# Two transformer blocks under a list scheduler: a longer assumed load time, finer priority offsets, and a last output in two pieces

## The chip, the cores and the metric

The kernel runs on one core of one Trainium2 chip. A core has TensorE (PE) for matmuls and transposes, VectorE (DVE), ScalarE (ACT), GpSimd (POOL), and SyncE (SP), which here issues nearly all DMA transfers. Every engine takes its instructions in a fixed order and waits on semaphores. The metric is the device time of one execution in microseconds.

## The reference, cut to what matters

The input is 256 tokens of 1024 columns, batch 1, float32. It goes through two layers of a first block and then two layers of a second one.

```python
# first block, per layer
mod = silu(c) @ w_ada[l] + b_ada[l]                  # 6 x 1024
hdn = modulate(rmsnorm(x, norm1_g[l]), shift1, scale1)
proj = hdn @ w_in[l]     # q_lat 768, c_kv 256, k_pe 32, sb_qkv 1536, mb_qkv 1536, gates 3072
q  = rmsnorm(q_lat) @ w_uq[l];  kv = rmsnorm(c_kv) @ w_ukv[l]
o_mla = softmax attention with rope;  o_sb = stick-breaking attention;  o_mb = block attention
merged = g_a * (o_mla @ w_o_mla) + g_b * (o_sb @ w_o_sb) + g_c * (o_mb @ w_o_moba)
x = x + gate1 * (merged @ w_out[l])
x = x + gate2 * (relu(modulate(rmsnorm(x, norm2_g[l])) @ w_ff1[l])**2 @ w_ff2[l])   # d_ff 4096
# then a final rmsnorm. Second block, per layer: modulation of x and of a context (256 tokens),
# one input projection, then branches for attention, Fourier, convolution and pooling over the
# tokens, concatenated to `cat`, and x = x + gate * (cat @ w_out_2[l]); the last layer ends with x.
```

## The kernel before, in words

Every float32 matmul is done as three matmuls of split operands: `mm3` multiplies high by high, high by low and low by high parts. A weight tile goes through three steps in `wload` (L600): a DMA into `raw`, a cast on ACT into `whi`, and a subtraction on DVE into `wlo`. PE then reads `whi` and `wlo`. Modulation vectors are made by "fillers" (`filler_step`, L752): loads `araw` and accumulations `acc` on DVE, let in between the weight loads at the rate `RATE`.

The Python code doesn't issue instructions. It records operations (`Recorder.add`, L228), and a list scheduler (`class Scheduler`, L320) gives each a start time and each tile a slot in SBUF (40 large, 11 half, 40 small) or PSUM (4 and 4 banks). `emit` (L444) then writes them out by start time, and so the order of each engine's instructions is set. All instructions carry its line: L464 before, L454 after. The scheduler's `forward` takes the ready operation with the smallest priority number. An operation's priority is its latest start in the last `backward` pass less its `lead`, an offset from the table `LEAD` (L1785) by `part` and `stage` of the code that recorded it (the stages are named `lat`, `up`, `att sb`, `gates`, `ff` and so on, with the layer's number). `LAG` (L329) is what the scheduler adds between an operation on an engine and one that needs its result. Its times are its own; the chip keeps only the orders.

Names used below: `sq_lat` and `lat` are the square sums and copies of the latent projections `g`; `ssv_ql` and `xn_ql` are the norm's small steps on DVE, and `nT_ql`, `nT_kvl` the transposes of the normed latents on PE. `s_sb`, `p_sb`, `pT_sb`, `pTs_sb` are scores, weights, transposed weights and their copies in stick-breaking attention. `gc` is a gate projection. `f`, `fr`, `f1T` are feed-forward products, the relu on ACT and their transposes. `tl_zc`, `cy` and `ct` are the convolution branch on DVE, and `cat0h`, `cat0l` its split result. `yt` and `gh` belong to the Fourier branch. The last product is `ev` in the second layer (L1700 to L1719): each 512 output columns of a token tile are multiplied by the gate, added to `x` and sent out by one DMA.

Of the kernel before, what the change touches and what calls it, by code (L numbers as in the profile page):

```python
# [18 lines left out]
ALU = mybir.AluOpType  # L19
# [148 lines left out]
class Recorder:  # L168
# [61 lines left out]
    def add(self, eng, fn, args, kw):  # L230
        if self.group:
            op = self.group[0]
        else:
            op = Op(len(self.ops), eng, fn, args, kw)
            op.lead = 0.0 if eng == "sync" else LEAD.get(self.part, 0.0) + LEAD.get(self.stage, 0.0)
            self.ops.append(op)
            if self.group is not None:
                self.group.append(op)
# [81 lines left out]
class Scheduler:  # L320
# [7 lines left out]
    LAG = {"tensor": 200.0, "vector": 150.0, "scalar": 150.0, "gpsimd": 100.0, "sync": 1000.0}  # L328
# [95 lines left out]
    def run(self, passes):  # L424

        best = None
        prio = list(range(len(self.ops)))
        for _ in range(passes):
            t = self.forward(prio)
            if best is None or t < best[0]:  # L430
                best = (t, [(op.start, op.end) for op in self.ops], [b.slot for b in self.bufs], self.edges)
            prio = [t - op.lead for t, op in zip(self.backward(), self.ops)]
        self.restore(best)
        return best[0]

    def restore(self, state):
        for op, (s, e) in zip(self.ops, state[1]):
            op.start, op.end = s, e
        for b, s in zip(self.bufs, state[2]):
            b.slot = s  # L440
        self.edges = state[3]
# [61 lines left out]
def record(nc, a, out):  # L503
# [102 lines left out]
    def wload(w2d, r0, nk, c0, n, eng=None, sort=0):  # L606


        uid[0] += 1
        parts = []  # L610
# [19 lines left out]
        filler_tick(nk * n / 2048.0)  # L630
        return parts
# [120 lines left out]
    def filler_step():  # L752
        nc.stage, stage = "ada", nc.stage
        try:
# [3 lines left out]
        nc.stage = stage  # L758
# [677 lines left out]
    def second_layer(l, late, hT):  # L1436
# [281 lines left out]
        gemm_tok(cat, 8, a["w_out_2"][l], [(512, 512)], lambda t, _, p: ev(t, 1, p), toks=toks, stag=True)  # L1718
        return h_next  # L1719
# [57 lines left out]
    for l in range(L):  # L1777
# [7 lines left out]
PASSES = 3  # L1785
RATE = 0.4354
LEAD = {"norm": 2550.0, "lead": 2700.0, "lead weights": 2950.0, "residual": -1660.0, "sb": -8810.0, "ml": -16600.0,
# [48 lines left out]
```

## Time and profile before

| | us |
|---|---|
| three runs | 1307.62, 1313.01, 1315.68 (median 1313.01) |
| the profiled execution | 1312.1 |
| its span, first to last instruction | 1310.1 |
| PE busy | 1270.7 (97%) |
| DVE busy | 1044.5 (80%) |
| ACT busy | 727.0 (55%) |
| POOL busy | 85.0 (6%) |

The span is about 2 us shorter than the execution it belongs to. PE is busy nearly all the time, so what matters is where PE stood idle or ran at a lower clock, and what ended each such stretch. In the profile's windows PEclk is the granted clock of TensorE: 1.00 is its 2.4 GHz level and 0.50 its 1.2 GHz level.

### The profile page before, as it was taken

To read this page: it belongs to the slowest core of one execution; us is meant where nothing else is said; L and a number is where in the kernel's file an instruction comes from. 1 tells how busy PE (TensorE), PEld (TensorE's weight loads), DVE (VectorE), ACT (ScalarE), POOL (GpSimd) and SP (SyncE) were. 2 spreads that over 40 slices of the span, in tenths; PEclk is the share of its full clock that TensorE was granted. 3 is DMA by queue.
4 is the path that set the end of the run, shared out by engine and by line. 5 is a ranking of instruction groups with operands and counts; after the bars stand their busy time and mean duration, and the time that the engine had idled before them with its cause. 6 is when DMAs were issued, how large, how long until landed. Compare 5 with 4: busy or idle time off the path is not lost. (4 is left out here: it accounts for less than half of the span.)

```text
span 1310.1 us, 21962 instructions
## 1 busy us (share of the span) xinstructions
PE 1270.7 (97%) x8258; PEld 1116.8 (85%) x8258; DVE 1044.5 (80%) x1705; ACT 727.0 (55%) x1246; POOL 85.0 (6%) x112
## 2 busy tenths in 40 slices
PE   6899999999999999999999999999999999999998
PEld 4898888997889888999889988889888777788997
DVE  4878988977966676888788978988878769967875
ACT  6576756645654554677566556545645453335661
POOL 1000000110000000100001200000001014100120
PEclk9898999999999999999999999999999999999999
DMA  8966565676688856775666766887744314824631
GB/s 293 354 231 206 173 215 193 224 241 227 212 319 271 282 186 203 251 235 180 205 219 194 250 226 228 284 294 238 250 140 150 105 35 163 276 79 134 218 105 38
DMA packets 164192, 272.68 MB, mean 208 GB/s; under 512 B 26395, under 2 KB 57071, under 8 KB 164086
## 3 DMA queue, kind: packets, MB, share of 16 engines
q1 hardware_dynamic: 164086, 271.28, 61.8%
q8 instruction: 65, 1.06, 0.3%
q14 instruction: 41, 0.34, 0.1%
HBM read 270.11 MB, written 1.13 MB: 207 GB/s over the span
## 5 line engine op out<-in xcount | busy, mean ns | idle before, releaser
L464 ACT CAST whi<-raw 128x1024 fp32r<-128x1024 f32 (+3 forms) x354 | 351.8, 1014 | 247.3 <-DMA raw<-w_ff 44.0
L464 DVE TENSOR_TENSOR wlo<-raw,whi 128x1024 fp32r<-128x1024 f32 (+3 forms) x354 | 412.5, 1195 | 38.3 <-ACT whi L464 33.1
L464 DVE SCALAR_TENSOR_TENSOR acc<-araw,cT,acc 128x1024 f32<-128x1024 f32 x147 | 190.2, 1313 | 37.8 <-DMA araw<-w_ada 26.5
L464 PE MATMUL gc<-hT1h,whi 128*128 128x256 f32 x256 | 74.0, 289 | 0.0
L464 PE MATMUL gc<-hT1h,wlo 128*128 128x256 f32 x256 | 71.9, 281 | 0.0
L464 PE MATMUL gc<-hT1l,whi 128*128 128x256 f32 x256 | 71.9, 281 | 0.0
L464 PE MATMUL f<-fT0h,whi 128*128 128x256 f32 x192 | 54.2, 282 | 0.0
L464 PE MATMUL f<-fT1l,whi 128*128 128x256 f32 x192 | 54.1, 282 | 0.0
L464 PE MATMUL f<-fT1h,whi 128*128 128x256 f32 x192 | 54.0, 281 | 0.0
L464 PE MATMUL f<-fT1h,wlo 128*128 128x256 f32 x192 | 54.0, 281 | 0.0
L464 PE MATMUL f<-fT0l,whi 128*128 128x256 f32 x192 | 53.9, 281 | 0.0
L464 PE MATMUL f<-fT0h,wlo 128*128 128x256 f32 x192 | 53.8, 280 | 0.0
L464 PE MATMUL cb<-h20h,whi 128*128 128x512 f32 x128 | 53.6, 419 | 0.0
L464 PE MATMUL gc<-hT0h,whi 128*128 128x256 f32 x176 | 51.7, 294 | 0.0
L464 PE MATMUL cb<-h20h,wlo 128*128 128x512 f32 x128 | 50.5, 394 | 0.0
L464 PE MATMUL cb<-h20l,whi 128*128 128x512 f32 x128 | 50.4, 394 | 0.0
L464 PEld LDWEIGHTS gc<-hT1h,whi 128*128 128x128 f32 x256 | 48.4, 189 | 2.1 <-issue 1.9
L464 PE MATMUL gc<-hT0l,whi 128*128 128x256 f32 x176 | 49.4, 281 | 0.0
L464 PE MATMUL gc<-hT0h,wlo 128*128 128x256 f32 x176 | 49.3, 280 | 0.0
L464 PEld LDWEIGHTS gc<-hT1l,whi 128*128 128x128 f32 x256 | 48.4, 189 | 0.0
L464 PEld LDWEIGHTS gc<-hT1h,wlo 128*128 128x128 f32 x256 | 48.3, 189 | 0.0
L464 PE MATMUL g<-whi,hT1h 128*128 128x512 f32 (+1 forms) x112 | 43.4, 388 | 0.0
(643 smaller groups left out, 3834.9 us busy)
## 6 DMA issues: line engine op xcount, KB each, us to landing
raw<-w_ff SPq DMA_DIRECT2D x128, 512.0 KB
raw<-w_in SPq DMA_DIRECT2D x126, 512.0 KB
araw<-w_ada SPq DMA_DIRECT2D x96, 256.0 KB
araw<-w_ada SPq DMA_DIRECT2D x32, 512.0 KB
raw<-w_out SPq DMA_DIRECT2D x32, 512.0 KB
araw<-w_mod SPq DMA_DIRECT2D x64, 256.0 KB
raw<-w_in SPq DMA_DIRECT2D x24, 352.0 KB
araw_l<-lead_ada SPq DMA_DIRECT2D x32, 256.0 KB
```

The lines of the kernel that those rows point to most:

```text
L464: op.inst.append(getattr(getattr(nc, op.eng), fn)(*[val(x) for x in args], **{k: val(x) for k, x in kw.items()}))
```

## The change

The scheduler assumes 3932 ns between a load and its first reader where it assumed 1000. Loads get offsets too, an operation's offset is now the sum of those of its part, its stage and its stage on its engine, and the three steps of `wload` form a part "weights" of their own; fillers belong to no part. All offsets have new values. `run` makes five passes and keeps the last instead of the best of three, and `RATE` is a little higher. In the last layer the last 512 columns of the second token tile are computed, gated, added and sent out as two pieces of 256 columns (24 matmuls of 512 columns become 48 of 256; DVE gets two instructions more, SP one DMA more).

```diff
--- before.py
+++ after.py
@@ -232,7 +232,8 @@
             op = self.group[0]
         else:
             op = Op(len(self.ops), eng, fn, args, kw)
-            op.lead = 0.0 if eng == "sync" else LEAD.get(self.part, 0.0) + LEAD.get(self.stage, 0.0)
+            op.lead = 0.0 if eng == "sync" else sum(
+                LEAD.get(q, 0.0) for q in (self.part, self.stage, f"{self.stage}/{eng}"))
             self.ops.append(op)
             if self.group is not None:
                 self.group.append(op)
@@ -325,7 +326,7 @@
                 self.ops[p].succs.append(op.idx)
         self.bufs = rec.bufs
 
-    LAG = {"tensor": 200.0, "vector": 150.0, "scalar": 150.0, "gpsimd": 100.0, "sync": 1000.0}
+    LAG = {"tensor": 200.0, "vector": 150.0, "scalar": 150.0, "gpsimd": 100.0, "sync": 3932.0}
 
     def lag(self, a, b, raw=True):
 
@@ -423,22 +424,11 @@
 
     def run(self, passes):
 
-        best = None
         prio = list(range(len(self.ops)))
-        for _ in range(passes):
-            t = self.forward(prio)
-            if best is None or t < best[0]:
-                best = (t, [(op.start, op.end) for op in self.ops], [b.slot for b in self.bufs], self.edges)
-            prio = [t - op.lead for t, op in zip(self.backward(), self.ops)]
-        self.restore(best)
-        return best[0]
-
-    def restore(self, state):
-        for op, (s, e) in zip(self.ops, state[1]):
-            op.start, op.end = s, e
-        for b, s in zip(self.bufs, state[2]):
-            b.slot = s
-        self.edges = state[3]
+        for i in range(passes):
+            if i > 0:
+                prio = [t - op.lead for t, op in zip(self.backward(), self.ops)]
+            self.forward(prio)
 
 
 def emit(tc, ctx, rec):
@@ -607,6 +597,7 @@
 
 
         uid[0] += 1
+        nc.part, part = "weights", nc.part
         parts = []
         step = max(1, 1024 // n)
         for j in range(0, nk, step):
@@ -628,6 +619,7 @@
                 (eng or nc.vector).tensor_tensor(l_, r_, h_.bitcast(F32), op=ALU.subtract)
             parts.extend((hv[:, i], lv[:, i]) for i in range(m))
         filler_tick(nk * n / 2048.0)
+        nc.part = part
         return parts
 
 
@@ -751,11 +743,12 @@
 
     def filler_step():
         nc.stage, stage = "ada", nc.stage
+        nc.part, part = None, nc.part
         try:
             next(filler[0][1])
         except StopIteration:
             filler.pop(0)
-        nc.stage = stage
+        nc.stage, nc.part = stage, part
 
     def filler_tick(n):
         rate[1] += n * rate[0]
@@ -1715,8 +1708,20 @@
                     second_norm(l + 1, "c", xc[t - 2], ss[t], t, h_next)
 
         gemm_tok(cat, 8, a["w_out_2"][l], [(0, 512)], ev, toks=toks)
-        gemm_tok(cat, 8, a["w_out_2"][l], [(512, 512)], lambda t, _, p: ev(t, 1, p), toks=toks, stag=True)
-        return h_next
+        if full:
+            gemm_tok(cat, 8, a["w_out_2"][l], [(512, 512)], lambda t, _, p: ev(t, 1, p), toks=toks, stag=True)
+            return h_next
+
+        ws = wload(a["w_out_2"][l], 0, 4, 512, 512) + wload(a["w_out_2"][l], 512, 4, 512, 512)
+        for t, c0, n in ((0, 512, 512), (1, 512, 256), (1, 768, 256)):
+            p = MM(f"end{t}{c0}")[:, 0:n]
+            for k, (wh, wl) in enumerate(ws):
+                c = slice(c0 - 512, c0 - 512 + n)
+                mm3(p, cat.h(k)[:, tok(t)], cat.l(k)[:, tok(t)], wh[:, c], wl[:, c], k == 0, k == 7)
+            tmp, sl = S2(f"rt_end{t}{c0}", n), slice(c0, c0 + n)
+            nc.vector.tensor_tensor(tmp, p, gate_bc[("x", l)][:, sl], op=ALU.mult)
+            nc.vector.tensor_tensor(x[:, t, sl], x[:, t, sl], tmp, op=ALU.add)
+            nc.sync.dma_start(out=out[0, t * 128:(t + 1) * 128, sl], in_=x[:, t, sl])
 
 
     for l in range(L):
@@ -1782,16 +1787,48 @@
 
 SLOTS = {"s4": 40, "s2": 11, "sm": 40, "mm": 4, "tr": 4}
 CAPS = {"w": 24, "r": 8}
-PASSES = 3
-RATE = 0.4354
-LEAD = {"norm": 2550.0, "lead": 2700.0, "lead weights": 2950.0, "residual": -1660.0, "sb": -8810.0, "ml": -16600.0,
-        "mb": -6240.0, "attention2": -17800.0, "ada": 3060.0, "att mb0": -190.0, "att mb1": -1340.0,
...
-        "up1": 770.0, "z att0": 5800.0, "z att1": 620.0}
+PASSES = 5
+RATE = 0.4386
+LEAD = {"None/sync": -6220.0, "None/tensor": -670.0, "None/vector": -290.0, "ada/sync": 8040.0, "att mb0": -60.0,
+        "att mb0/scalar": 290.0, "att mb0/tensor": 2280.0, "att mb0/vector": 110.0, "att mb1": -690.0,
+        "att mb1/scalar": 660.0, "att mb1/tensor": -90.0, "att mb1/vector": -10.0, "att ml0/scalar": -2180.0,
...
+        "up1/vector": -2950.0, "z att0": -318.0, "z att0/scalar": 260.0, "z att0/sync": -3760.0,
+        "z att0/vector": 1350.0, "z att1": 40.0, "z att1/tensor": -500.0, "z att1/vector": -200.0}
```

Three places show how the orders move.

**Place 1: up0, the latent norm of the first layer.** PE, from the end of the latent projection `g` to the transposes `nT_ql` and `nT_kvl`. Before (the left-out rows repeat the pair of `s_sb`):

```order
L464 MATMUL g_10_1031<-whi_2_924,hT0l_513 128x352
L464 MATMUL s_sb_1133<-kssb_811,qssb_780 128x128
L464 MATMUL s_sb_1133<-k_low_73,qssb_780 128x128
...
L464 MATMUL nT_ql_1163<-ct,xn_ql_1151 128x128 x4
L464 MATMUL nT_ql_1172<-ct,xn_ql_1151 128x128 x2
L464 MATMUL nT_kvl_1188<-ct,xn_kvl_1161 128x128 x2
L464 MATMUL nT_kvl_1198<-ct,xn_kvl_1192 128x128 x2
L464 MATMUL g_00_1207<-whi_0_955,laT0h_1186 128x384
```

And now:

```order
L454 MATMUL g_10_1027<-whi_2_973,hT0l_514 128x352
L454 MATMUL s_sb_1120<-kssb_799,qssb_773 128x128 x3
L454 MATMUL gc_0_1124<-hT0h_198,whi_0_1078 128x256
L454 MATMUL gc_0_1124<-hT0l_205,whi_0_1078 128x256
L454 MATMUL gc_0_1124<-hT0h_198,wlo_0_1094 128x256
L454 MATMUL s_sb_1120<-kssb_799,qssb_773 128x128
L454 MATMUL gc_0_1124<-hT0h_198,whi_0_1078 128x256
L454 MATMUL gc_0_1124<-hT0l_205,whi_0_1078 128x256
L454 MATMUL gc_0_1124<-hT0h_198,wlo_0_1094 128x256
L454 MATMUL s_sb_1120<-k_low_75,qssb_773 128x128 x4
L454 MATMUL nT_ql_1157<-ct,xn_ql_1137 128x128 x4
L454 MATMUL nT_ql_1164<-ct,xn_ql_1137 128x128 x2
```

Two groups of three `gc` stand among the eight `s_sb` ahead of `nT_ql`. ACT at the same place, up to the square sums and copies of that projection. Before (`whi_0_1029` is a cast for the product behind the norm, `gt` a gate activation):

```order
L464 CAST whi_0_1029<-raw_0_1003 128x768
L464 ACTIVATE sq_lat_1040,sl_13_1041<-g_11_978 128x352
L464 ACT_TABLE_LOAD
...
L464 COPY lat_1055<-g_11_978 128x352
L464 CAST whi_0_1079<-raw_0_1043 128x2x256 x2
L464 CAST whi_0_1097<-raw_0_1064 128x2x256 x2
L464 ACTIVATE sq_lat_1115,sl_14_1116<-g_00_1025 128x64
```

And now:

```order
L454 CAST whi_0_1060<-raw_0_986 128x2x256 x2
L454 CAST whi_0_1078<-raw_0_1007 128x1024
L454 ACT_TABLE_LOAD
L454 ACTIVATE rope_c<-rope_c 128x48
L454 CAST whi_2_1096<-raw_2_1025 128x768
L454 ACTIVATE sq_lat_1106,sl_14_1107<-g_00_1018 128x64
...
L454 COPY lat_1016<-g_10_1027 128x320
L454 CAST whi_0_1153<-raw_0_1044 128x768
```

The cast `whi_0_1029` of before is `whi_0_1153` now, and stands behind the last copy `lat` instead of ahead of the square sums. Ahead of the first of these square sums are now a cast in two pieces, one of 1024 columns, a table load with the `rope_c` activation, and one of 768 columns. The order of ACT has 9 table loads where it had 8.

**Place 2: the convolution branch of the second block's first layer.** DVE, up to the first `tl_zc`. Before:

```order
L464 SCALAR_TENSOR_TENSOR cy_12472<-tl_cc_12343,vt,cy_12472 128x2x255 x2
L464 TENSOR_TENSOR wlo_2_12495<-raw_2_12410,whi_2_12443 128x1024
L464 TENSOR_TENSOR wlo_0_12505<-raw_0_12420,whi_0_12470 128x1024
L464 TENSOR_TENSOR wlo_2_12517<-raw_2_12436,whi_2_12497 128x1024
L464 TENSOR_TENSOR wlo_0_12529<-raw_0_12457,whi_0_12510 128x1024
L464 SCALAR_TENSOR_TENSOR acc_0_12382<-araw_2_12512,cT,acc_0_12382 128x1024
L464 SCALAR_TENSOR_TENSOR tl_zc_12556<-th_zc_12548,cb_2048_0_12438 128x512
L464 SCALAR_TENSOR_TENSOR tl_zc_12556<-th_zc_12558,cb_2048_1_12445 128x512
```

And now:

```order
L454 SCALAR_TENSOR_TENSOR cy_12468<-tl_cc_12337,vt,cy_12468 128x2x255 x2
L454 TENSOR_TENSOR wlo_0_12482<-raw_0_12363,whi_0_12431 128x1024
L454 TENSOR_TENSOR wlo_2_12495<-raw_2_12380,whi_2_12466 128x1024
L454 TENSOR_TENSOR wlo_0_12507<-raw_0_12390,whi_0_12490 128x1024
L454 TENSOR_SCALAR acc_0_12514<-araw_0_12426,cT 128x1024
L454 TENSOR_TENSOR wlo_2_12519<-raw_2_12403,whi_2_12500 128x1024
L454 SCALAR_TENSOR_TENSOR tl_zc_12540<-th_zc_12529,cb_2048_0_12442 128x512
L454 SCALAR_TENSOR_TENSOR tl_zc_12540<-th_zc_12542,cb_2048_1_12447 128x512
```

The order at the place is almost the same; an accumulation with a multiply and add has become one with a multiply alone. By the operations counted from the start, tl_zc is row 1281 of DVE's order and was row 1289.

**Place 3: stick-breaking attention in the second layer.** ACT, from the copy of one transposed weight tile to that of the next. Before:

```order
L464 COPY pTs_sb_7005<-pT_sb_6988 128x512
L464 ACTIVATE gt_6986<-gc_1_6721 128x512
L464 COPY rr_7017<-rs_7000 128x256
L464 COPY pTs_sb_7026<-pT_sb_7013 128x512
L464 CAST whi_2_7029<-raw_2_6843 128x1024
L464 CAST osb1h_6978<-pv_sb_7031 128x512
```

And now:

```order
L454 COPY pTs_sb_6633<-pT_sb_6624 128x512
L454 CAST whi_2_6642<-raw_2_6443 128x1024
L454 CAST whi_0_6661<-raw_0_6567 128x1024
L454 CAST whi_0_6678<-raw_0_6462 128x1024
L454 CAST whi_2_6700<-raw_2_6480 128x1024
L454 CAST whi_2_6709<-raw_2_6622 128x1024
L454 CAST osb1h_6722<-pv_sb_6687 128x512
L454 CAST whi_0_6727<-raw_0_6644 128x1024
L454 COPY mkT_6742<-kn_6601 64x2x256
L454 COPY pTs_sb_6755<-pT_sb_6744 128x512
```

Before, a gate activation and a small copy stood between the last two copies `pTs_sb`; now six casts of weights and two other instructions do.

## Rows read from the trace of the kernel before

**Rows 1.** the page, busy time, share of the span and instructions of each engine
```profile
PE 1270.7 (97%) x8258; PEld 1116.8 (85%) x8258; DVE 1044.5 (80%) x1705; ACT 727.0 (55%) x1246; POOL 85.0 (6%) x112
```

**Rows 2.** windows: length, busy us of PE, PEld, DVE, ACT, POOL; PEclk, DMA share, GB/s
```profile
8.70:58.50 49.80, 43.63 (x293) 35.59 (x293) 38.17 (x84) 27.77 (x42) 0.56 (x1) 0.97 0.94 331
...
99.50:106.30 6.80, 5.38 (x20) 4.51 (x21) 5.56 (x18) 4.21 (x9) 1.94 (x4) 0.50 0.28 92
106.30:1041.60 935.30, 924.00 (x6168) 825.05 (x6167) 760.14 (x1136) 537.99 (x883) 38.72 (x46) 1.00 0.67 223
1041.60:1045.00 3.40, 3.40 (x10) 2.64 (x9) 2.70 (x8) 1.41 (x4) 0.00 (x0) 0.50 0.02 5
```

**Rows 3.** PE's waits, 58 us to the end: released by; us in total, times, longest
```profile
PE nT_ql L464 <- DVE ssv_ql L464: 3.6, 1, 3.6
PE pT_sb L464 <- DVE p_sb L464: 2.5, 3, 1.6
PE g L464 <- DVE tl_zc L464: 2.5, 1, 2.5
PE f1T L464 <- ACT fr L464: 2.1, 2, 1.5
PE yt L464 <- ACT gh000s L464: 1.9, 1, 1.9
PE ld L464 <- ACT hT0h L464: 1.7, 1, 1.7
PE nT_c L464 <- DVE xn_c L464: 1.1, 2, 0.6
```

**Rows 4.** timeline of ACT: start, us, instruction, idle before and its releaser
```profile
87.86 0.84 ACT L464 CAST whi<-raw 128x768 fp32r<-128x768 f32 x1 [1.69 <-DMA raw<-w_uq]
...
91.02 0.84 ACT L464 CAST whi<-raw 128x768 fp32r<-128x768 f32 x1 [1.28 <-DMA raw<-w_uq]
...
92.33 1.28 ACT L464 ACT_TABLE_LOAD   x1
...
95.74 2.33 ACT L464 CAST whi<-raw 128x512 fp32r<-128x512 f32 x4
98.05 0.22 ACT L464 ACTIVATE sq_lat<-g 128x64 f32<-128x64 f32 x1
```

**Rows 5.** timeline of ACT and PE at f1T
```profile
345.07 1.05 ACT L464 CAST whi<-raw 128x1024 fp32r<-128x1024 f32 x1 [0.30 <-DMA raw<-w_ff]
...
346.02 0.59 ACT L464 ACTIVATE fr<-f 128x512 f32<-128x512 f32 x1
...
346.67 0.66 PE L464 MATMUL f1T<-ct,fr 128*128 128x128 f32 x4 [1.54 <-ACT fr L464]
```

**Rows 6.** timeline of DVE ahead of tl_zc
```profile
1137.58 5.72 DVE L464 TENSOR_TENSOR wlo<-raw,whi 128x1024 fp32r<-128x1024 f32 x4
1143.23 1.27 DVE L464 SCALAR_TENSOR_TENSOR acc<-araw,cT,acc 128x1024 f32<-128x1024 f32 x1
```

**Rows 7.** ACT's waits over the span: us in total, times, longest
```profile
ACT whi L464 <- DMA raw<-w_in: 42.4, 21, 9.2
```

**Rows 8.** timeline of the last instructions, PE and DVE
```profile
1305.16 0.40 PE L464 MATMUL g<-wlo,cat1h 128*128 128x512 f32 x1
...
1305.39 0.39 PE L464 MATMUL g<-whi,cat1l 128*128 128x512 f32 x1
1305.82 0.69 DVE L464 TENSOR_TENSOR rt_x<-g,gate_x 128x512 f32<-128x512 f32 x1 [2.07 <-PE g L464]
1306.55 0.69 DVE L464 TENSOR_TENSOR x<-x,rt_x 128x512 f32<-128x512 f32 x1
```

**Rows 9.** groups of DVE's instructions: a 128x256 operand in PSUM
```profile
L464 DVE TENSOR_TENSOR s_mb<-s_mb,ct 128x256 f32<-128x256 f32 x8 | 3.4, 429 | 1.6 <-PE s_mb L464 1.6
```

**Rows 10.** timeline of PE, two 128x256 matmuls in a row
```profile
1269.59 0.28 PE L464 MATMUL cb<-h21h,whi 128*128 128x256 f32 x1
1269.71 0.28 PE L464 MATMUL cb<-h21l,whi 128*128 128x256 f32 x1
```

More of the change, by code (lines that the diff above doesn't have):

```diff
@@ L1784 @@
 CAPS = {"w": 24, "r": 8}
-PASSES = 3
-RATE = 0.4354
-LEAD = {"norm": 2550.0, "lead": 2700.0, "lead weights": 2950.0, "residual": -1660.0, "sb": -8810.0, "ml": -16600.0,
[7 rows of a table removed]
+PASSES = 5
+RATE = 0.4386
+LEAD = {"None/sync": -6220.0, "None/tensor": -670.0, "None/vector": -290.0, "ada/sync": 8040.0, "att mb0": -60.0,
[16 rows of a table added]
+        "lead": 3119.0, "lead weights": 2070.0, "mb": -1510.0, "ml": -12100.0, "norm": 2550.0, "out mb0": -2320.0,
[22 rows of a table added]
 @with_exitstack
```

39 rows, old and new, of the table LEAD are left out of this document.

## The prediction, made before the changed kernel was run

> **What bounds the kernel now.** I read the engine shares first, then TensorE's waits, then its clock by stretch, and then the neighbours of each long wait. PE is busy 1270.7 us of a span of 1310.1 us, DVE 1044.5 us [rows 1]. The reader should see that a new order can win only where PE stands idle or runs slowly: 1310.1 - 1270.7 = 39.4 us of idle time, of which 8.75 us lie ahead of the first matmul. The opening to 58.5 us moves 331 GB/s at a DMA share of 0.94 [rows 2]. It waits for bytes, and since the change leaves the bytes as they are, and the order of loads there nearly so, I cost it at nothing.
>
> From 58 us to the end PE waited for a result 21.3 us in all, in 18 rows, of which the seven largest are shown [rows 3]. The row of `ld` (1.7 us, and a further one of 0.6) belongs to the opening, so 19.0 us are left. After some of these waits the clock was lower: from 99.5 to 106.3 us the granted clock was 0.50, the 1.2 GHz level, with 5.38 us of PE work, and from 1041.6 to 1045.0 us again, with 3.40 us [rows 2]. At the 2.4 GHz level that work takes half, so the two stretches cost 2.7 and 1.7 us. Over the 935 us between them the clock was 1.00. An end of all this is near: 19.0 + 4.4 = 23.4 us, and the tail.
>
> **The change, part by part.** The five passes, the longer load time, the offsets and the rate cost nothing by themselves; they act through the order alone. No operation of the middle is added or removed, so the sum is one of waits.
>
> *Up0* (place 1). PE waited 3.6 us at `nT_ql` [rows 3] and 0.8 at `nT_kvl` (one of the smaller rows). ACT was late there: it took the first square sum at 98.05 us, after a weight cast that waited 1.28 us for its load and took 0.84, a table load of 1.28, and four casts in 2.33 us [rows 4]. The order now moves the cast that waited behind the square sums. From the cast at 87.86 us [rows 4] on, ACT now has that cast (0.84), two copies (about 0.6 each, an estimate), two pieces of 128x512 (half of 2.33, 1.17), one of 1024 columns (1.05, rows 5), a table load (1.28), the small activation (about 0.3, an estimate) and a cast of 768 columns (0.84): 6.7 us, which ends at 94.6 instead of 98.05. PE also has six `gc` more ahead of `nT_ql`, at 0.12 us each [rows 10] 0.7 us. Both together cover 3.45 + 0.7 = 4.1 of the 4.4. The bound from below is that the two larger loads, now ahead, land late: then only PE's 0.7 less the 0.3 that ACT's work grows by (1.28 for the table load, 1.0 less of casts), 0.4 us. I take **3.3**, nearer to the upper end because the cast that showed the load wait has left the path.
>
> The table load is the point where I weigh a rule. In the trace the load starts at 92.33 us, takes 1.28, and is over at 93.61 with the next activation at 93.62 [rows 4]. The Trainium skill ("ScalarE: Activation LUTs", section "What ACT_TABLE_LOAD costs") gives the load 1283 ns, which agrees, and adds a drain of some 1380 ns to every switch, which this trace does not show. By the page the extra load would take 1.4 us more from ACT here, and the sum would come out 1.4 us later at most.
>
> *The clock behind it.* With the gap at 96.5 to 100.0 us gone, I let the low stretch after it go too: **2.7**. It could also come elsewhere (see the second rival). The stretch after 1041.6 us I keep: the order there is nearly as tight as before.
>
> *Stick-breaking attention of the first layer*, `pT_sb`, 2.5 us in three waits [rows 3]: in the new order 4 us and more of other matmuls stand ahead of each of these transposes, so **2.3**.
>
> *Feed-forward*, `f1T`, 2.1 us [rows 3]: a cast on ACT (345.07 to 346.02 us) stood ahead of `fr`, and PE had six matmuls of 256 columns to bridge it [rows 5]. Now ACT has two casts there where it had three, and PE has two transposes more. Each alone is worth up to 1.05 us [rows 5], and one wait of two goes in full: **1.6**, with 0.3 and 2.1 as ends.
>
> *Convolution*, `tl_zc`, 2.5 us [rows 3] (place 2). DVE works without a break up to it, four `wlo` in 5.72 us and an `acc` of 1.27 [rows 6]. At the same place of PE's order DVE now has 8 instructions less behind it, 3.8 us by their durations in the trace. **2.2**, with 0.5 (one `acc` with a multiply alone) and 2.5 as ends.
>
> *The rest.* `nT_c` and `nT_x` (1.9): the order stands 1 to 3 us of matmuls more ahead of them, **1.4**. A `g` that waits for `mT0h` (1.1): **0.9**. `yt` (1.9): half, **0.9**, since its margin stays some 0.3 us. Seven smaller rows, 2.6 us: **0.8**.
>
> *The tail.* After the last matmul (1305.39 us) DVE multiplies and adds 512 columns, 0.69 us each [rows 8], and the DMA follows. For 256 columns a DVE instruction with an operand in PSUM takes 0.43 us [rows 9], so the two take 0.26 us less each, 0.5 us; the output's transfer is half as large, and the first half's work runs under the second's matmuls. The matmuls themselves: 24 steps of 0.23 us [rows 8] are 5.5 us, 48 steps of 0.12 us [rows 10] are 5.8. Together **0.6**, with 0 and 1.2 as ends.
>
> *New waits.* The new order is tight in new places: place 3, two late transposes of the MLA and block attention in the first layer, and the latent attention of the second block's second layer, which ends later in the order than it did. The waits of before are the nearest prices: 0.5 to 3.6 us each [rows 3]. I take four at 0.5, **-2.0**, with 0 and -12 as ends.
>
> Sum: 3.3 + 2.7 + 2.3 + 1.6 + 2.2 + 1.4 + 0.9 + 0.9 + 0.8 + 0.6 - 2.0 = 14.7 us. The profiled execution took 1312.1 us, so 1297.4; the median of the three runs shown is 0.9 above it, and they lie 8 us apart. I predict **1297.5 us**.
>
> **The rivals.**
>
> *The waits move and do not go.* ACT and DVE stay in order, the loads come no earlier (SP still waits for the same kind of buffer), and each wait that closes lets PE run into the next late result. For it speaks that DVE is 80% busy [rows 1] and that the seven places are fed by the same casts. Against it: of the places in the order where less than 0.3 us stands between a result's chain and its reader, few are left. It gives back 9 to 15 of the 14.7 us: 1306 to 1312 us. Chance 0.25.
>
> *Slower: weight casts ahead of attention copies.* At place 3 six casts stand between two copies `pTs_sb`; at 1.05 us each [rows 5] they take 6.3 us if their data are there. A cast that waits for a load holds the copy, PE's `pv` behind it, and all of ACT; the longest such wait of before was 9.2 us [rows 7]. With a low clock after it, as after 99.5 us (2.7 us), one such place costs up to 12 us. It decides if loads land later than ACT reaches them by more than PE's cover, which the longer assumed load time speaks against. It takes one full place beyond the gain to be slower than before: 15 us for one and a half of them gives 1312, and three places 1334. Chance of any time over 1313: 0.10, over 1326: 0.05.
>
> *All of it goes.* 19.0 of waits, 4.4 of clock and 1.2 at the tail: 1312.1 - 24.6 = 1287.5; with fewer waits in the opening as well 1284. Chance 0.13.
>
> *The change does not do what it says.* SP waits for free buffers, not for the scheduler's clock, so a longer load time could leave the chip's order of loads as it was and the offsets shift only what was hidden. Then only the tail is left: 1311.5. Against it stands place 1, which did move. Chance 0.05.
>
> **How the numbers follow.** My forecast has the remaining 0.47; its own range is 1291 to 1304, from the ends of up0, the convolution and the new waits. About 1% is what a measurement of this kernel can tell from no change, so faster is below 1299.9 us: all of the third rival and 0.43 of the forecast, 0.56. Slower is above 1326: 0.05. Within 1%: 0.39. The range of 8 in 10 leaves out the slower rival (0.10) and half of the third and the upper edge of the first (0.10): 1286 to 1310.
>
> **What would show it.** In the profile after: no wait above 1 us at `nT_ql` and a granted clock of 1.00 from 99 to 106 us (up0); no row of `pT_sb` on `p_sb` in the first layer; `f1T` and `tl_zc` under 0.6 us; PE's idle time after 58 us under 10 us; the first square sum of place 1 on ACT within 1 us of PE's end of `g`. The last DVE addition would take some 0.43 us. It would be wrong if PE's waits keep their sum under other names, above all as ACT copies behind `whi` casts, or if low clock stretches show up at new places.

## The result, and the profile after

The changed kernel takes **1279.24 us** (median of 4 runs, 1278.47 to 1279.97); the kernel before took 1313.8 us beside it (4 runs, 1307.62 to 1315.68). The ratio is 0.9745 [0.9711, 0.9778]. The forecast was 1297.5 us with a range of 1286 to 1310: the direction was right, and of a gain of about 34 us I had accounted for 14.7.

One correction to the section on the change: loads get no offset that acts. The new table has entries for SP, but `Recorder.add` gives every operation on SP a lead of zero, and without those entries the order of every engine is the same.

The page's first row, after. Against [rows 1], PE is 15.2 us less busy although it has 24 matmuls more: busy time holds the time at the low clock and short waits too.

```profile
PE 1255.5 (98%) x8282; PEld 1112.8 (87%) x8282; DVE 1043.1 (82%) x1707; ACT 726.0 (57%) x1247; POOL 85.2 (7%) x112
```

Three windows from the first matmuls to near the end, after (columns as in [rows 2]; the clock is the column ahead of the last two). It reads 1.00 in all three, where the kernel before had four stretches at 0.50 in that time, two of them in the opening (17.6 and 58.5 us) and the two of [rows 2].

```profile
8.70:58.50 49.80, 45.56 (x305) 38.33 (x306) 38.65 (x84) 27.24 (x42) 0.56 (x1) 1.00 0.98 343
58.50:1041.60 983.10, 980.38 (x6572) 880.92 (x6572) 818.79 (x1271) 588.44 (x994) 42.75 (x54) 1.00 0.66 224
1041.60:1276.00 234.40, 229.59 (x1409) 193.54 (x1407) 185.30 (x352) 104.79 (x203) 37.63 (x42) 1.00 0.43 143
```

PE's waits from 58 us to 1310 us, after (us in total, times, longest). All rows together are 5.7 us in 12 waits; before they were 19.0 in 20 without `ld` [rows 3]. Of the seven largest rows of before, `pT_sb`, `f1T`, the `g` on `tl_zc` and `ld` are gone, `nT_ql` has 0.4 left of 3.6, and `nT_c` alone has grown.

```profile
PE nT_c L454 <- DVE xn_c L454: 1.5, 1, 1.5
PE g L454 <- DVE qssb L454: 0.7, 1, 0.7
PE nT_c L454 <- ACT sq L454: 0.7, 1, 0.7
PE nT_kvl L454 <- ACT p_sb L454: 0.6, 1, 0.6
PE nT_x L454 <- DVE xn_x L454: 0.5, 1, 0.5
PE nT_ql L454 <- DVE ssv_ql L454: 0.4, 1, 0.4
...
PE yt L454 <- ACT gh000s L454: 0.2, 1, 0.2
```

Timeline of ACT at place 1, after (start, us, instruction). Against [rows 4], the first square sum starts at 91.31 instead of 98.05 us, and no cast ahead of it waits for its load. PE starts the last matmul of the projections `g` at 91.24; the tile squared first had its own last one six matmuls earlier, at 90.27.

```profile
86.98 2.15 ACT L454 CAST whi<-raw 128x512 fp32r<-128x512 f32 x3
89.14 1.28 ACT L454 ACT_TABLE_LOAD   x1
90.44 0.24 ACT L454 ACTIVATE rope_c<-rope_c 128x48 f32<-128x48 f32 x1
90.59 0.82 ACT L454 CAST whi<-raw 128x768 fp32r<-128x768 f32 x1
91.31 0.22 ACT L454 ACTIVATE sq_lat<-g 128x64 f32<-128x64 f32 x1
```

The end of the timeline, after. Against [rows 8], the last multiply and addition take 0.42 and 0.43 us instead of 0.69 each.

```profile
1274.17 0.28 PE L454 MATMUL end<-whi,cat1l 128*128 128x256 f32 x1
1274.49 0.42 DVE L454 TENSOR_TENSOR rt_end<-end,gate_x 128x256 f32<-128x256 f32 x1 [1.94 <-PE end L454]
1274.95 0.43 DVE L454 TENSOR_TENSOR x<-x,rt_end 128x256 f32<-128x256 f32 x1
```

**A view that I had not read** is the waits of PE's weight loads. Two matmuls of 256 columns start 0.12 us apart and each is shown 0.28 long [rows 10]; a start that comes 0.16 us late leaves no idle time in PE's row. The row of weight loads can show such waits. First before, then after, 66 us to the end (released by; us in total, times, longest):

```profile
PEld f1T L464 <- ACT fr L464: 5.1, 8, 1.7
...
PEld nT_ql L464 <- issue: 3.7, 1, 3.7
...
PEld g L464 <- DVE tl_zc L464: 2.9, 1, 2.9
PEld yt L464 <- ACT gh000s L464: 2.3, 1, 2.3
PEld pT_sb L464 <- ACT gt L464: 1.8, 1, 1.8
```

```profile
PEld pv L454 <- ACT pTs_l L454: 1.9, 6, 0.4
PEld nT_c L454 <- issue: 1.9, 1, 1.9
...
PEld f1T L454 <- ACT fr L454: 1.0, 5, 0.2
```

The waits of this row for ACT or DVE were 37.6 us in 67 before, and are 13.8 in 39 after. `f1T` had 5.1 in 8 where PE's row showed 2.1 in 2 [rows 3].

**Where the time came from.** For each matmul I took the time to the next one's start, less the median of its form in the kernel before, and sorted what is over. Idle: visible gaps above 0.1 us after 65 us. Edge: what the interval that holds such a gap takes beyond the gap and its median, since the matmul ahead of a gap counts at its full length (0.28 us, not the 0.12 to a next start). Short: all other excess at full clock. Low clock: excess in stretches at half the clock, after 65 us. Opening: the first matmul's start and all excess up to 65 us. End: from the last matmul's start on.

| us, one profiled execution each | opening | idle | edge | short | low clock | end | span |
|---|---|---|---|---|---|---|---|
| before | 26.8 | 18.7 | 4.1 | 35.2 | 5.8 | 4.7 | 1310.1 |
| after | 22.4 | 5.9 | 2.3 | 28.5 | 0 | 4.0 | 1278.2 |
| gain | 4.4 | 12.7 | 1.8 | 6.7 | 5.8 | 0.7 | 31.9 |
| before, load time 3932 | 22.1 | 10.7 | 3.2 | 36.3 | 2.7 | 4.7 | 1294.7 |
| after, load time 1000 | 27.9 | 16.5 | 3.8 | 32.6 | 1.5 | 4.0 | 1301.5 |
| before, load time 6000 | 21.5 | 16.3 | 4.5 | 36.8 | 6.0 | 4.7 | 1304.6 |
| before, casts swapped | 24.9 | 41.3 | 6.0 | 35.5 | 14.2 | 4.7 | 1341.4 |

The gains add up to 32.1. Some of the experiments below leave an order as it was over a long stretch, and their profiles tell how far one execution can be trusted:

- *Behind 65 us.* The order of before stands in three profiles (before, and the experiments on the opening and the new end): idle 18.7 to 20.6, edge 4.1 to 4.7, short 35.0 to 35.8, low clock 3.1 to 7.1. That of the changed kernel stands in three too (after, unaltered again, old end): 5.1 to 5.9, 2.1 to 2.3, 28.4 to 28.5, and 0. So idle, edge and short belong to the order, and the low clock's price varies.
- *The opening.* Up to 65 us the order of before stands in five profiles, with 23.5 to 26.8 us (mean 25.5), and the changed one in six, with 20.5 to 23.0 (mean 22.1). So by the means about 3.4 of the 4.4 belong to the order. The low-clock stretches in the opening of before can't be priced in this spread: the new end's profile, with none there, took 26.7 us.
- *Short* is what is left over, and not all of it is shown to be waits. Of its 6.7 us, 2.6 stand in intervals at whose end the weight load waits for ACT or DVE (43 of them before, 31 after), 0.8 where the trace names something else as the end of its wait, and 3.3 where no wait is shown at all.

### The profile page after: what moved, and what is told of

It reads as the page before. It is cut to its first block, busy times and chain, and to the rows that moved or that the text cites. A ratio compares the mean times of both kernels' runs of the same rounds, so it can differ in the third digit from the quotient of the medians.

```text
span 1278.2 us, 22019 instructions
## 1 busy us (share of the span) xinstructions
PE 1255.5 (98%) x8282; PEld 1112.8 (87%) x8282; DVE 1043.1 (82%) x1707; ACT 726.0 (57%) x1247; POOL 85.2 (7%) x112
## 4 chain that ended last, share of the span: by engine, by line
PE 88%; DMA 4%; DVE 3%; issue 2%; ACT 1%; SPq 1%; POOL 0%; ACTq 0%; POOLq 0%
PE gc L454 17%; PE g L454 16%; PE f L454 14%; PE ff L454 13%; PE cb L454 11%; PE qkvp L454 3%; DMA wraw_l<-lead_w 2%; PE ufp L454 1%; DMA araw_l<-lead_ada 1%; PE rs L454 1%; PE end L454 1%; DMA raw<-w_in 1%; PE pv L454 1%; PE s_l L454 1%; PE pT_l L454 1%
## 5 line engine op out<-in xcount | busy, mean ns | idle before, releaser
L454 DVE TENSOR_TENSOR wlo<-raw,whi 128x1024 fp32r<-128x1024 f32 (+2 forms) x354 | 407.8, 1184 | 57.5 <-ACT whi L454 32.6
```

The costliest lines, as they stand in the source:

```text
L454: op.inst.append(getattr(getattr(nc, op.eng), fn)(*[val(x) for x in args], **{k: val(x) for k, x in kw.items()}))
```

## The experiments

The theory after the result: PE's waits for ACT and DVE, short ones included, fell because loads land before ACT and DVE reach their readers. ACT waited 132.5 us for loads in 71 waits before, and 11.5 in 9 after; DVE 54.7 in 33, and 0.6 in 1. The rival: the places at which a result is tight ahead of its reader in the order are fewer, by the offsets, and the load waits are a side effect. In the short diffs below `move` puts operations of one engine behind another of it and `swap` exchanges neighbours; all other orders stay unless the text says so.

**The opening** (before, altered):

```diff
+    move(rec, "vector", ("posf", "ang"), "hT0l1", 2)
+    move(rec, "scalar", ("whi_l70", "whi_l71024"), "nt_n106")
```

> The kernel before, with one move at 55 us: on DVE the position cast posf and two ang steps go behind hT0l, on ACT two weight casts whi_l go behind hT0h and nt_n; everything else as before. Theory (the order of the opening, not its bytes, cost time): PE's gap of 2.2 us at 55.7 to 58.7 us shrinks to 0.6 or less, the low clock stretch of 58.5 to 65.4 us (3.4 us lost) does not come, and the time falls by 4 to 5.5 us. Rival (the opening waits for bytes): the gap moves to a later load, and the time stays within 1 us. Rival (the low clock comes by itself): the gap goes and the stretch stays, so 1.5 to 2.2 us.

1308.69 us (8 runs), ratio 0.9968 [0.9947, 0.999]: 3.4 us less than the kernel before beside it, where 4 to 5.5 were expected. In the kernel before a cast on ACT waits for its load ahead of `hT0h`, a tiny cast of the positions on DVE waits for its load ahead of `A_n`, which `hT0h` needs, and PE stands (timeline of before; the bracket is the idle time ahead and its releaser):

```profile
54.69 1.92 ACT L464 CAST whi_l<-wraw_l 128x1024 fp32r<-128x1024 f32 x2 [4.70 <-DMA wraw_l<-lead_w]
...
56.40 0.17 DVE L464 CAST posf<-pos_i 128x2 f32<-128x2 int32 x1 [1.27 <-DMA pos_i<-positions]
...
56.87 0.15 DVE L464 SCALAR_TENSOR_TENSOR A_n<-modT_a,vt 128x1 f32<-128x1 f32 x1
...
57.72 0.39 PE L464 MATMUL ld<-hT0h,whi_l 128*128 128x256 f32 x1 [1.66 <-ACT hT0h L464]
```

With both moved, the same instructions come 2.4 us earlier (timeline of this kernel):

```profile
54.49 0.15 DVE L464 SCALAR_TENSOR_TENSOR A_n<-modT_a,vt 128x1 f32<-128x1 f32 x1
...
55.34 0.38 PE L464 MATMUL ld<-hT0h,whi_l 128*128 128x256 f32 x1 [0.29 <-ACT hT0h L464]
```

The last `g` of 352 columns, ahead of up0, starts at 91.09 us instead of 95.30 (after: 91.24). But with the opening of before it starts anywhere from 91.86 to 95.30 us in five profiles (mean 93.9), so one pair says too much. By the mean, and by the time, the opening did not only wait for bytes: about 3 us of it was the order.

**Up0** (before, altered): the four cast pieces that stood ahead of the square sums go behind a later copy, with the two subtractions on DVE that read two of them, and one load stays behind them.

```diff
+    move(rec, "scalar", ("whi12_0", "whi13_0"), "lat01", 2)
+    move(rec, "vector", ("wlo12_0",), "laT0l1", 1)
```

> The kernel before, with one move at 96 us: four pieces of weight casts on ACT (2.33 us) go behind the square sums and copies, and the two subtractions that read two of them go behind the first latent results on DVE. Theory: the wait at nT_ql falls from 3.6 to 1.2 to 1.6 us. If the low clock stretch behind it (99.5 to 106.3 us, 2.7 us lost) hangs on the length of the gap, it goes as well and the time falls by 4 to 5 us in all; if the stretch comes by itself, 2 us. A rival that ACT's share was not what held nT_ql: under 0.5 us.

1308.96 us (10 runs), ratio 0.9973 [0.9947, 0.9999]: 3.1 us less, between the 2 expected with a low stretch left and the 4 to 5 without. `nT_ql` fell from 3.57 to 0.52 us, but `nT_kvl` now waited 1.3 in two waits and a `g` 0.99 for `laT0h`: the wait moved in part, and a stretch of 3.4 us at the low clock stayed at 98.5 us.

**f1T, from both sides.** Before with each group of `f1T` transposes one group of `f` matmuls later, and after with each one group earlier:

```diff
# before, altered: each group behind one more f group
+            for k, t in enumerate(line[i:j]):
+                t.start = line[j].start + 0.001 * (k + 1)
# after, altered: each group one f group earlier
+            swap(line, i - 1, i, j - i)
```

> The kernel before, with each of the eight groups of transposes f1T moved behind one more group of three f matmuls on PE. PE's idle row of f1T was 2.1 us in 2 waits; its weight loads waited 5.1 us in 8. Theory that short waits cost time which the idle row does not show: all eight waits of the weight loads shrink, their sum falls by 3 us or more, and the intervals from an f to an f1T that were 3.4 us over the usual fall under 1.2, so 2 to 2.5 us. Theory that only idle counts: 0.7 to 1.2 us.

> The changed kernel with each of the eleven groups of transposes f1T on PE one group of three f matmuls earlier, nothing else. Six of them had 0.71 to 0.93 us of matmuls between the product and the transpose, against a relu of 0.60 us, so the cover goes to 0.2 to 0.4. Theory that short waits cost what the idle row does not show: the intervals from f to f1T grow by 2 to 3.5 us and the time with them, while PE's idle row of f1T shows 1.0 to 2.0. Theory that only idle counts: the time grows as the idle row does.

The first: 1308.92 us (7 runs), ratio 0.9951 [0.993, 0.9972]. The excess of the intervals from `f` to `f1T` and between `f1T` fell from 3.82 to 1.26 us, while PE's own row of it fell only from 2.1 to 0.9. The time by itself is no proof, since these runs also had a higher clock. The second: 1283.07 us (1282.8 to 1283.32), ratio 0.9774, 4.0 above the changed kernel run beside it, at a clock of 1.0. PE's wait, in this kernel:

```profile
PE f1T L454 <- ACT fr L454: 3.4, 6, 0.7
```

It was nothing in the changed kernel, and the weight loads' wait rose from 1.0 to 5.6. The excess of the same intervals rose by 4.5 us (0.21 to 4.73). So waits of at most 0.7 us are paid in full. But 1.0 to 2.0 us were expected in PE's own row, and with 3.4 there most of it was visible: the run says little of waits that this row hides. The first run does: 2.6 us of excess went and 1.2 of visible wait.

**The clock behind a gap** (after, altered: one weight cast of up0 is done five times):

```diff
+    cast.calls = cast.calls * 5
```

> The changed kernel with one weight cast on ACT ahead of the first latent square sum done five times instead of once (four more of 0.84 us), nothing else. Theory: the gap at nT_ql, 0.43 us, becomes 3.4 to 3.8; with the gap a low clock stretch of the kind of before returns behind it in some or all executions. The time goes up by 3.2 us for the wait and 1.7 to 3.4 more where the stretch comes, 3 to 7 in all, and the mean clock falls by 0.001 to 0.003. Rival (stretches do not follow gaps): 3.2 us and the clock of the changed kernel. Rival (ACT's work there is covered): under 1 us.

1283.76 us (1282.08 to 1285.26), ratio 0.9779. The gap at `nT_ql` is back, and with it the stretch (timeline of PE, then windows of this kernel):

```profile
96.78 1.51 PE L454 MATMUL nT_ql<-ct,xn_ql 128*128 128x128 f32 x6 [3.87 <-DVE ssv_ql L454]
```

```profile
92.00:95.30 3.30, 0.90 (x9) 0.76 (x7) 0.41 (x3) 2.95 (x7) 0.02 (x1) 0.99 0.17 61
95.30:102.10 6.80, 5.32 (x26) 5.36 (x26) 4.97 (x17) 4.50 (x13) 2.45 (x5) 0.50 0.00 0
102.10:1276.00 1173.90, 1169.98 (x7708) 1035.99 (x7708) 967.18 (x1548) 657.90 (x1129) 77.87 (x91) 1.00 0.62 207
```

PE was busy for 0.90 of 3.30 us, then the clock was 0.50 for 6.8 us, with 5.32 us of work, 2.7 us lost. That is the price of the prediction's term, and the mean clock was 0.997 in all four runs. The time is 4.7 us above the changed kernel beside it (3 to 7 were expected): the wait at `nT_ql` grew by 3.4 us, but PE's waits from 58 us on only by 2.5 (5.7 to 8.2), since the wait at `nT_kvl` behind it is gone and one at `nT_c` is shorter.

All profiles bear it out. In the nine with the longest waits at `nT_ql` (1.8 to 3.9 us) a stretch at 0.50 begins within 2.5 us of it; in the nine others (1.7 us or less) none does.

**The end**: the new end on the kernel before, and the old end on the changed one.

```diff
+        for t, c0, n in ((0, 512, 512), (1, 512, 256), (1, 768, 256)):
```

> The kernel before, with the last 512 columns of the second token tile in two pieces as in the change, and the scheduler and its numbers as before. Theory: the end behind the last matmul falls from 4.3 to 3.75 us, as it did in the change, and the time by 0.5 to 0.8 us, plus or minus 2 for the order that the scheduler draws anew. Rival (the tail is a main part of the gain): 5 us or more at the tail.

> The changed kernel with the last columns in one piece as before. The order ahead of the tail is that of the change. Theory: the end behind the last matmul is 4.7 us instead of 4.0, and the time 0.5 to 0.8 us higher than the changed kernel's 1279.1. Rival (the tail carries a main part): 5 us or more.

1309.82 us (10 runs), ratio 0.9983 [0.9954, 1.0013], and 1279.44 us (1277.89 to 1280.21), ratio 0.9751 [0.972, 0.9782]. By the trace the end behind the last matmul's start is 4.71 us old and 4.01 new in both kernels. 0.7 us can't be told from nothing in the time.

**The load time alone**, on the kernel before, and back on the changed one; and the rate back.

```diff
# before: 3932.0, 2000.0 and 6000.0; after: 1000.0 and 6000.0
-    LAG = {..., "sync": 1000.0}
+    LAG = {..., "sync": 3932.0}
# after
-RATE = 0.4386
+RATE = 0.4354
```

> The kernel before with 3932 ns for a load and nothing else. 18 tight places by the same count. Theory: within 6 us of before, 1305 to 1314. Rival (the longer load time is the part that wins): 1290 or less.

> The changed kernel with 1000 ns for a load as before; offsets, passes and tail as in the change, so the scheduler draws another order. Counted in the order with the trace's durations, places where less than 0.3 us stand between a result's chain and its reader on PE: 20 before, 5 in the change, 13 here. Theory (the gain is the waits that the order leaves): 33 us over 15 places, so about 1279 + 8 x 2.2 = 1297, between 1288 and 1304. Rival (a longer load time itself lets loads land earlier): near 1310. Rival (the load time is nothing): 1280.

> The changed kernel with the filler rate of before, 0.4354 instead of 0.4386, and all else as in the change. The order is drawn anew; 9 tight places by the same count. Theory: 1279 + 4 x 2.2 = 1288, between 1282 and 1294: a number that moves three fillers costs part of the gain, since the table was fitted to one order. Rival (the offsets carry over to another order): within 2 us of 1279.

This one number makes the kernel before **1297.08 us** (1295.88 to 1297.73), ratio 0.9883 [0.9856, 0.9909], and without it the changed kernel takes **1302.16 us**, 0.9921 [0.9893, 0.9949]. My expectation for the first, a time within 6 us of before, missed by far. ACT's waits for loads fell to 16.7 us and rose to 149.1. The old rate on the changed kernel costs 6.6 us: 1285.83, 0.9799 [0.9769, 0.9828].

ACT's waits for loads, before with 3932 (all of them), and the two largest of PE's waits after with 1000:

```profile
ACT whi L464 <- DMA raw<-w_in: 12.2, 8, 4.3
ACT whi L464 <- DMA raw<-w_ff: 4.5, 4, 1.7
```

```profile
PE f1T L454 <- ACT fr L454: 4.4, 2, 2.7
PE pT_sb L454 <- DVE p_sb L454: 2.6, 3, 2.0
```

The table of the section above says what moved. The load time alone gave back opening, idle time and clock, and none of the short excess (36.3); all else of the change with the old load time gave 2.5 us of it. Both together give 6.7. The count of tight places, made before each run, was right for the changed kernel with 1000 ns and with the old rate (1288 to 1304 and 1282 to 1294 were expected) and wrong for this one: 18 tight places, two less than before, and 15 us less time. So neither theory had all of it.

**Load waits taken off ACT and DVE, with PE's order left alone** (before, altered: the 57 casts and 29 accumulations that had waited 0.3 us or more for loads, one of them twice, each go behind the next instruction of another kind on their engine):

```diff
+            swap(line, i, j, 1)
```

> The kernel before, with 57 weight casts on ACT and 30 accumulations on DVE, those that waited 0.3 us or more for their load in the trace of before, each moved behind the next instruction of another kind on its engine. PE's and SP's orders are as before. Theory (they stood ahead of their loads and held what was behind them): ACT's waits for loads fall from 132 to under 100 us, DVE's from 55 to under 35, PE's weight loads wait less, and the time falls by 4 to 10 us. Rival (those waits are covered, and only the drawn order counts): within 3 us of before.

**1343.71 us** (1339.68 to 1344.01), ratio 1.0263 [1.0221, 1.0304]. ACT's waits for loads fell from 132.5 to 28.0 us and DVE's from 54.7 to 28.4, and the kernel became 2.6% slower. PE's waits from 66 us on were 40.7 us instead of 19.0, the largest of them:

```profile
PE g L464 <- DVE tl_zc L464: 8.7, 1, 8.7
PE tt_mb L464 <- ACT p_ml L464: 5.1, 1, 5.1
PE tt_mb L464 <- DVE rp_mb L464: 4.6, 1, 4.6
PE pT_sb L464 <- DVE p_sb L464: 4.1, 4, 1.8
```

The theory that load waits on ACT and DVE are the cost by themselves falls. The likely reason is that a cast that is put off comes late for its own reader; that it helps where PE's order is made for it fits the runs with 3932 and was not tried by itself.

**Other load times:**

> The kernel before with 2000 ns for a load. Theory (dose): ACT's waits for loads between 132 and 17 us, some 60 to 90, and a time between the two, 1301 to 1309 us. Rival (each redraw is chance): no order among 1000, 2000, 3932 and 6000.

> The kernel before with 6000 ns for a load. Theory: ACT's waits for loads at 17 us or less, so no more to win there: 1293 to 1300 us, as with 3932. Rival (chance): anything from 1290 to 1312.

> The changed kernel with 6000 ns for a load. In the drawn order 13 places have less than 0.3 us between a result's chain and its reader, as many as with 1000 ns, where the time was 1302. Theory that waits for loads are what 1000 ns costs: they stay under 20 us on ACT here, and the time is 1280 to 1290. Theory that the tight places in the order alone set the time: 1293 to 1304.

Before with 2000: 1305.86 us, 0.9979 [0.9958, 0.9999]. Before with 6000: 1306.8, 0.9978 [0.9959, 0.9997]. After with 6000: 1293.76, 0.989 [0.9852, 0.9927]. With 6000 ACT's waits for loads are 4.0 us in the one and 0 in the other, yet PE waits for results again. After with 6000:

```profile
PE qkvp L454 <- DVE wlo L454: 3.7, 1, 3.7
PE nT_ql L454 <- DVE ssv_ql L454: 1.8, 1, 1.8
PE pT_l L454 <- DVE p_l L454: 1.8, 1, 1.8
```

The first row is a late subtraction of a weight tile: it looks as if the readers of loads are now placed so late that their own readers wait, which the other rows don't show. My expectations that less load wait is a lower time missed twice; the count of tight places had the last one right (1293 to 1304). Of the times tried, 3932 is the best with both tables of offsets.

**Unaltered again, and a version to beat both.** The second moves five late transposes (`nT_c`, `nT_kvl`, `nT_x`, `nT_ql`) one or two groups of matmuls later.

```diff
+    for names, k in ((("nT_c120", "nT_c124"), 2), (("nT_c130", "nT_c134"), 1), (("nT_kvl010",), 2),
+                     (("nT_x110", "nT_x114"), 1), (("nT_ql000", "nT_ql004", "nT_kvl000"), 1)):
```

> The changed kernel once more, unaltered, as the base for the runs beside it. Theory that the low clock stretches of before come out of its gaps on PE: the changed kernel, whose longest gap after the opening is 1.5 us, shows mean clocks of 0.996 or more in every execution and times of 1277 to 1283 us. Rival (the stretches are chance and the four executions so far were lucky): clocks of 0.989 to 0.995 in some, and times up to 1290.

> The changed kernel with five groups of transposes on PE one or two groups of matmuls later, where it still waited: nT_c (1.5 and 0.66 us), nT_kvl (0.63), nT_x (0.53), nT_ql (0.43). Theory: these 3.7 us of idle fall to 1.2 or less and the time falls by 2 to 3 us, 0.15 to 0.25%. Rival (the waits move to the next reader): within 1 us.

1279.07 us (1278.01 to 1280.47), ratio 0.9744 [0.9713, 0.9776], and 1277.72 (1277.21 to 1279.15), 0.9732 [0.9695, 0.9769]. The last is the fastest run here, by 1.4 us where 2 to 3 were expected, and the ranges overlap. PE's waits show why it is not more:

```profile
PE nT_c L454 <- ACT sq L454: 1.3, 1, 1.3
PE nT_c L454 <- DVE xn_c L454: 0.8, 1, 0.8
...
PE ufp L454 <- DVE wlo L454: 0.5, 1, 0.5
```

One `nT_c` wait grew (0.7 to 1.3) as the other shrank (1.5 to 0.8), and a new one came at `ufp`.

**One row for the time.** Over the 18 profiles of this case the median time follows 1263.5 + 1.244 x (us that PE's weight loads wait for ACT or DVE, 66 us to the end), with a correlation of 0.98 and a scatter of 3.2 us; with PE's own waits the scatter is 4.6. It is a description of these 18, not a law.

## Why the prediction was wrong

**Its end was the step that failed.** It said "An end of all this is near: 19.0 + 4.4 = 23.4 us, and the tail", and so no rival went below 1284. The waits in PE's row were rightly read and rightly taken: 12.7 us of idle time went, where the eight terms for waits and the new waits made 11.4. Every sign that it named came true: `nT_ql` under 1 us, the clock at 1.00, the rows of `pT_sb`, `f1T` and `tl_zc` gone, 5.7 us of waits behind 58 us, the square sum within 1 us of PE's `g`, the last addition at 0.43. They test the waits alone, and so could not show what the sum left out. Missing were three things that PE's row of waits does not hold.

1. **Edges of gaps and short excess, 8.5 us** (1.8 and 6.7), cost at nothing. Of this 4.4 is tied to waits: the edges, and 2.6 us where a weight load is shown to wait for ACT or DVE. A sign of it stood in the weight loads' row, 37.6 us against 19.0 in PE's, and `f1T` shifted one group later shows that such waits cost more than PE's row says. The other 4.1 us belong to the order too, but that they are waits is not shown.
2. **The clock, 5.8 us instead of 2.7.** The stretch behind up0 went as forecast, and the gap put back brought it back. But I kept the one after 1041.6 us, and it went too. The two other profiles with the order of before lose 7.1 and 3.1 us, so the term is some 3 to 7. By PE's busy time the two are 2.7 and 1.7 us [rows 2]; by the starts of the matmuls, which count what stands between them as well, they are 5.8 together. In the 26 executions of the kernel before that stand beside the first four experiments, the mean clock was 0.989 to 0.997 and the time 1304.1 to 1318.4 us, some 1.23 us for each 0.001; drawn on to the 0.999 of the changed kernel, beyond all of them, that line gives 1304.0, 8 us less than their median. It counts the opening too, and whatever comes with a low clock. I could not bring the two ways to one number.
3. **The opening, 4.4 us, cost at nothing.** "It waits for bytes" was read from a DMA share of 0.94 [rows 2]. The share is a mean: at its end two casts whose results are needed late waited for their loads ahead of two instructions that PE needed. The experiment took 3.4 us by moving four names, and 3.4 is also what the means of several profiles leave of the 4.4.

The terms add up: the forecast's 14.7, and 1.3 more of idle time, 8.5, 3.1, 4.4 and 0.1 at the end make 32.1. This holds for the two profiles; over several the opening is nearer to 3.4 and the clock is 3 to 7.

**Term by term.** *Up0*: 3.3 us forecast; `nT_ql` 3.57 to 0.43 and `nT_kvl` 0.79 to 0.63 make 3.3. The first square sum starts 0.1 us behind the start of PE's last `g` matmul; before it was 2.8 (98.05 against 95.30). On the rule weighed there, the Trainium skill ("ScalarE: Activation LUTs", "What ACT_TABLE_LOAD costs") says that a switch also drains the engine for some 1380 ns. After, the load at 89.14 us takes 1.28 and the next activation starts at 90.44; the nine loads are 11.5 us in all, with 1.1 us of idle time ahead of them:

```profile
L454 ACT ACT_TABLE_LOAD x9 | 11.5, 1283 | 1.1 <-PEq L1864 0.7 <-DVE s_sb L454 0.2
```

The measurement decides: no drain here. *`pT_sb`, `f1T`, `tl_zc`, `mT0h`*: their rows are gone, right at the upper ends. The "8 instructions less" of DVE at `tl_zc` don't show in the traces: 1447 stand ahead of it where 1450 did, 3.5 us less by their durations. *`yt`*: 1.9 to 0.4 (two rows of 0.2), where half was forecast. *`nT_c` and `nT_x`*: forecast to lose 1.4 of 1.9; they rose to 2.7. These were the wrong ones: more matmuls ahead of a transpose are no gain if its chain on ACT and DVE has been put later too, which I take to be the reason and did not test. *New waits*: forecast 2.0 in four places; outside `nT_c` and `nT_x` they make 1.4 in four small ones, 0.7 the longest. *The end*: 0.6 forecast, 0.7 by the trace.

**"The five passes, the longer load time, the offsets and the rate cost nothing by themselves; they act through the order alone."** That may be true and is of no use: the load time alone gives 15 us, undone it takes 23, and I had no price for it. A view that pointed to it was at hand: 132.5 us of waits for loads on ACT, of which the prediction showed one row [rows 7] and used it only against the change. It was no price, though: the swapped casts show that such waits can go and the time still rise.

**The rivals.** The waits did not move: 12 small ones are left. The slower rival asked for a `pv` behind casts at place 3; there is no such wait, and the longest wait of ACT for a load is 3.5 us:

```profile
ACT whi L454 <- DMA raw<-w_ff: 9.2, 5, 3.5
```

"All of it goes" was nearest, and still 5 us too high.

**What stays open.** Why 3932 is better than 2000 and 6000 on the kernel before (by 9 and 10 us), and than 6000 on the changed one (by 15). The two agree, but each number draws a new order, and the rate, less than 1% lower, moved the time by 6.6 us, so that a part of it may be the draw. What the new offsets do, against the passes, was not tried apart. Nor is it settled what a low stretch in the opening costs, nor what the 3.3 us of short excess are at whose places no wait is shown.

## What to carry to other kernels

Where one engine is 97% busy, take the room for gain from the starts of its instructions, not from its idle time: the excess of each interval over the median of its form, with the waits in the weight loads' row beside it. In a scheduled kernel an assumed latency is a size like any other: ask what waits for loads stand on the helper engines, but judge a change by the reader's waits, since taking load waits away in place can cost more than they did. And look at several executions before a low stretch or an opening gets a price.

## What the hardware showed that I had not expected

Some stretches at the 1.2 GHz level stay with the order, and others come and go between executions of the same order. The one behind the wait at `nT_ql` stands in all three profiles that have the order of before from there on: at 99.5 us, at 100.7 with the new end, at 93.9 with the opening altered. The others don't: besides it the kernel before had stretches at 17.6, 58.5 and 1041.6 us, the new end none up to the last matmul, and the altered opening at 646.9 and 1039.4. They were 3.4 or 6.8 us long; the kernel before with 6000 ns had one of 10.2, at 1182.3 us.

The times of the kernel before spread by 14.3 us in 26 executions, and those of the changed one by 2.5 in 8. The number of gaps does not explain that: with 6000 ns the kernel before has 28 gaps above 0.1 us behind 65 us, more than its 24, and its ten times lie within 1.8 us.
